# A kernel of seven-product projections on one Trainium2 core: another order of the products, x loaded by quarters, 1/rms moved into the functions, and branch work fed among the units

## The chip, the cores and the metric

The kernel runs on one core of one Trainium2 chip. The metric is the device time of one execution in microseconds (us). The figure for a kernel is the median of several runs; one further execution was taken with a profile, and every row below is from that one.

## What is computed

`x` is 512 tokens by 2048 channels, float32. It is normalised, projected by one large matrix, mixed in three branches, merged by gates, projected again and added to `x`:

```python
h = rmsnorm(x, norm_g)
a_u, a_b, a_c, a_z, b_v, b_g, b_z, c_u, c_z, gates = split(h @ w_in)   # nine of 1024 columns, gates 3 x 2048
y_a = (silu(a_z) * a_b * conv3(a_c * a_u)) @ w_br_a
v   = silu(layernorm(conv31(b_v * sigmoid(b_g)) + conv_b, ln_g, ln_b))
y_b = (silu(b_z) * v) @ w_br_b
y_c = (silu(c_z) * pool_mix(c_u) * scale) @ w_br_c                      # causal means of 2, 4, 8, 16
g   = sigmoid(gates)
x   = x + (g[0] * y_a + g[1] * y_b + g[2] * y_c) @ w_o
return rmsnorm(x, final_g)
```

## The kernel before

**Arithmetic.** Every matmul operand is split in a high part (rounded to the matmul's format) and a low part (the rest), and a product is three matmuls: high-high, low-high, high-low (L338, L339, L340 in a unit). Weights arrive as raw blocks of 128 x 1024. ScalarE (ACT) casts the high part `wh` (L125), VectorE (DVE) subtracts to get the low part `wl` (L126), both in halves of 512 columns.

**Units.** The input projection is cut into 15 units, each giving two column groups of 512. A unit computes a 2 x 2 block product by seven products instead of eight, named 11, s1, s2, s4, s3, 12 and 22 (`PRODUCTS`, L54). Each product runs over eight k, and at each k issues three matmuls to each of two PSUM banks: 48 matmuls a product, 336 a unit, all of 512 columns. Some blocks of raw weights are plain loads on SyncE's queue ("load", L105); others are added into the block before by an accumulating DMA that GpSimd issues ("add", L110). In the order before, the blocks that s1, s2 and s3 add to were begun four stages (of 1024 columns) earlier.

**Accumulation over products.** 11 is computed in the banks X, copied out by ACT (`snap`, L351), and s2 goes on in the same X; its sum is copied out, s3 goes on in X, and so does 22. s1 and s4 share the banks Z in the same way. Where a bank's contents are taken out, DVE's `join` (L360) or ACT's `snap` reads it before PE may write on. In the order before there is always a whole other product between two products on the same banks: 11 (X), s1 (Z), s2 (X), s4 (Z), s3 (X), 12 (V), 22 (X). 1/rms is applied as the scale of `snap` and `join`.

**Operands of x.** The seven left operands are built during unit 0 (`make`, L275, called by `run` at each k): x is loaded as 16 tiles `xa`, `xb` on SyncE's queue, scaled by `norm_g` on ACT, and combined and split on DVE. The token squares for 1/rms are loaded and summed in unit 0 too, since the first `join` needs 1/rms.

**What sets the order.** A queue of tasks (`todo`, and `urgent` ahead of it) holds all the other work: turning results to channels, the 31-tap convolution, LayerNorm, pooling. `feed` (L221) is called at each k of the products and hands out a number of tasks per call (`rate`). A scheduler then orders the instructions on each engine by priority; the split of weights has a high priority (L124). Each engine executes its queue in order.

**After the units.** Three branch products (`branch`, L633; branch 0 is y_a, 2 is y_c, 1 is y_b) and the output product `o`, whose last column group runs token block by token block (L829). The operands of branch 0 (`ua`) are loaded and halved after the last unit (L659 to L662); pooling and its mixing run as tasks during branch 0, the product silu(z)·v during branch 2. The units' order is glu, prod and side, pool, the six gate units, and `zed` last.

## Time and profile before

| | us |
|---|---|
| median of three runs | 1697.19 (1694.49 to 1698.14) |
| the profiled execution, its own time | 1691.05 |
| its span in the profile | 1689.3 |
| TensorE (PE) busy | 1642.6 (97%) |
| DVE busy | 1126.3 (67%) |
| ACT busy | 823.6 (49%) |

The span is the time from the first to the last instruction in the profile; the execution's own time has 1.75 us around it. PE's share says that almost all of the span is matmuls, and so the few per cent that are idle, or run at the lower clock, are where a change of schedule can act. The profile also gives the clock that TensorE was granted, as a share of its 2.4 GHz: 0.50 is 1.2 GHz.

### The profile page before, as it was taken

How to read it: one execution, taken by the hardware profiler on the slowest of the kernel's cores; microseconds unless marked ns; L12 is line 12 of the kernel's file. 1: busy time of each engine (PE TensorE's matmuls, PEld its weight loads, DVE VectorE, ACT ScalarE, POOL GpSimd, SP SyncE). 2: the span in 40 equal slices, each digit the busy share in tenths (PEclk: the TensorE clock that was granted, in tenths of full speed). 3: DMA queues.
4: the chain of work that ended last, by engine and by line, in shares of the span. 5: the costliest groups of instructions: out<-in, count | busy, mean ns of one | idle time of the engine just before them, and what ended most of it. 6: DMA issues, size and time to landing. Idle time of an engine off the chain costs nothing.

```text
span 1689.3 us, 21512 instructions
## 1 busy us (share of the span) xinstructions
PE 1642.6 (97%) x7332; PEld 1353.5 (80%) x7332; DVE 1126.3 (67%) x1873; ACT 823.6 (49%) x1436; POOL 208.3 (12%) x246
## 2 busy tenths in 40 slices
PE   5899999999999999899999999999899999999997
PEld 4688888888888888688888888888688888888886
DVE  4859989969987986775555555555666754453442
ACT  7855544544545555565555555555533322332332
POOL 1212111120302021212112030212000000000000
PEclk7999999999999999999999999999999999999999
DMA  9979898897989899999899898989854854443312
GB/s 313 224 217 202 214 217 174 198 235 198 169 228 208 239 225 272 259 272 223 220 224 214 235 203 236 203 239 215 284 168 130 287 182 145 128 131 100 89 61 100
DMA packets 114589, 341.31 MB, mean 202 GB/s; under 512 B 12720, under 2 KB 12848, under 8 KB 114480
## 3 DMA queue, kind: packets, MB, share of 16 engines
q0 software_dynamic: 34560, 125.84, 40.0%
q1 hardware_dynamic: 59616, 177.24, 32.8%
q10 hardware_dynamic: 20304, 36.87, 6.2%
q8 instruction: 57, 0.93, 0.2%
q14 instruction: 52, 0.43, 0.1%
HBM read 306.35 MB, written 33.55 MB: 201 GB/s over the span
## 4 chain that ended last, share of the span: by engine, by line
PE 92%; DMA 5%; DVE 1%; ACT 1%; issue 1%; SPq 0%; ACTq 0%; DVEq 0%
PE X L338 12%; PE X L339 12%; PE X L340 12%; PE Z L338 6%; PE Z L340 6%; PE Z L339 6%; PE y L642 5%; PE y L644 5%; PE y L643 5%; PE V L340 3%; PE V L338 3%; PE V L339 3%; PE o L810 3%; PE o L812 3%; PE o L811 3%; PE turned L431 2%
## 5 line engine op out<-in xcount | busy, mean ns | idle before, releaser
L126 DVE TENSOR_TENSOR wl<-rawA,wh 128x512 fp32r<-128x512 f32 x560 | 379.7, 687 | 263.3 <-ACT wh L125 227.8
L125 ACT CAST wh<-rawA 128x512 fp32r<-128x512 f32 x560 | 342.4, 621 | 393.3 <-PE X L339 88.9
L126 DVE TENSOR_TENSOR wl<-rawB,wh 128x512 fp32r<-128x512 f32 x320 | 217.9, 688 | 178.5 <-ACT wh L125 146.2
L125 ACT CAST wh<-rawB 128x512 fp32r<-128x512 f32 x320 | 196.1, 622 | 266.3 <-PE y L643 67.4
L110 POOL DMA_DIRECT2D rawA<-wts x180 | 155.7, 865 | 851.7 <-DVE wl L126 810.0
L338 PE MATMUL X<-wh,x 128*128 128x512 f32 x480 | 188.8, 396 | 14.3 <-ACT wh L125 10.8
L338 PE MATMUL X<-wh,xs 128*128 128x512 f32 x480 | 189.3, 394 | 11.5 <-ACT snap L351 5.8
L338 PE MATMUL Z<-wh,xs 128*128 128x512 f32 x480 | 187.4, 393 | 3.3 <-ACT xs L269 3.1
L339 PE MATMUL X<-wh,xs 128*128 128x512 f32 x480 | 188.4, 393 | 0.0
L339 PE MATMUL X<-wh,x 128*128 128x512 f32 x480 | 187.9, 392 | 0.0
L339 PE MATMUL Z<-wh,xs 128*128 128x512 f32 x480 | 187.6, 391 | 0.0
L340 PE MATMUL Z<-wl,xs 128*128 128x512 f32 x480 | 172.9, 391 | 0.8 <-DVE wl L126 0.8
L340 PE MATMUL X<-wl,x 128*128 128x512 f32 x480 | 172.2, 394 | 0.0
L463 DVE SCALAR_TENSOR_TENSOR conv<-v,prm,conv 128x511 f32<-128x511 f32 (+28 forms) x240 | 171.4, 727 | 0.0
L340 PE MATMUL X<-wl,xs 128*128 128x512 f32 x480 | 170.6, 393 | 0.1
L338 PEld LDWEIGHTS X<-wh,x 128*128 128x128 f32 x480 | 90.9, 190 | 34.6 <-ACT wh L125 12.0
L338 PEld LDWEIGHTS X<-wh,xs 128*128 128x128 f32 x480 | 91.1, 190 | 33.0 <-ACT wh L125 8.1
L125 ACT CAST wh<-rawC 128x512 fp32r<-128x512 f32 x120 | 71.5, 619 | 91.4 <-DMA rawC<-wts 43.4
L338 PEld LDWEIGHTS Z<-wh,xs 128*128 128x128 f32 x480 | 90.8, 189 | 22.9 <-ACT xs L269 3.5
L340 PEld LDWEIGHTS X<-wl,xs 128*128 128x128 f32 x480 | 90.8, 189 | 20.7 <-DVE wl L126 1.8
L340 PEld LDWEIGHTS Z<-wl,xs 128*128 128x128 f32 x480 | 90.6, 189 | 20.3 <-DVE wl L126 1.4
L339 PEld LDWEIGHTS X<-wh,xs 128*128 128x128 f32 x480 | 91.1, 190 | 18.9
(189 smaller groups left out, 2654.2 us busy)
## 6 DMA issues: line engine op xcount, KB each, us to landing
rawA<-wts POOLq DMA_DIRECT2D x180, 512.0 KB, 7.5
rawA<-wts SPq DMA_DIRECT2D x100, 512.0 KB, 4.4
rawB<-wts SPq DMA_DIRECT2D x100, 512.0 KB, 4.4
rawC<-wts SPq DMA_DIRECT2D x60, 512.0 KB, 4.2
rawB<-wts POOLq DMA_DIRECT2D x60, 512.0 KB, 7.1
g<-g SPq DMA_DIRECT2D x48, 256.0 KB, 4.4
g<-snap ACTq DMA_DIRECT2D x36, 256.0 KB, 4.0
xq<-xn SPq DMA_DIRECT2D x16, 256.0 KB, 7.2
```

The costliest lines, as they stand in the source:

```text
L110: self.nc.gpsimd.dma_start(out=t, in_=self.src[b], accum_op=ALU.add)
L125: self.nc.scalar.copy(out=h, in_=raw)
L126: self.nc.vector.tensor_tensor(out=l, in0=raw, in1=h.bitcast(F32), op=ALU.subtract)
L338: T.matmul(p, lhsT=xh, rhs=h, start=start and k == 0, stop=False, skip_group_check=True)
L339: T.matmul(p, lhsT=xl, rhs=h, start=False, stop=False, skip_group_check=True)
L340: T.matmul(p, lhsT=xh, rhs=l, start=False, stop=k == KB - 1, skip_group_check=True)
L463: V.scalar_tensor_tensor(out=c[:, s:], in0=v[:, : S - s], scalar=pcol(P_BW, i * CONV_B + CONV_B - 1 - s), in1=c[:, s:], op0=ALU.mult, op1= ...
L642: T.matmul(banks[t], lhsT=uh[:, tk], rhs=h, start=k == 0, stop=False)
L643: T.matmul(banks[t], lhsT=ul[:, tk], rhs=h, start=False, stop=False)
L644: T.matmul(banks[t], lhsT=uh[:, tk], rhs=l, start=False, stop=k == KB - 1)
L810: T.matmul(pt[t], lhsT=mh[:, tk], rhs=h, start=k == 0, stop=False)
L811: T.matmul(pt[t], lhsT=ml[:, tk], rhs=h, start=False, stop=False)
```

## The change

- `PRODUCTS` becomes 11, 12, s1, s4, s2, s3, 22. An added block now follows its predecessor by eight stages. The third pool of raw blocks is dropped, the second grows from 4 to 6.
- Weights are split by whole blocks of 1024 columns (the very first block in two pieces), two stages ahead; loads run four stages ahead instead of three.
- x comes by quarters (two k by 256 tokens): the two of the upper token half on ACT's queue at the start, the other two on SyncE's queue during the first products. Operands are built by pairs of k, up to four k ahead, with `norm_g` inside the instructions that split or subtract.
- 1/rms: `snap` is a plain copy, `join` a plain sum; the scale is applied in the sigmoids and products that follow. What follows the joins of unit 0 is put off to unit 1, where `roots` now runs; eight of the 16 squares move to unit 1.
- `feed` counts an estimate of VectorE's us per task: 0.5 us per k, 0.7 in the branches.
- `zed` comes ahead of the gate units. Pooling's mixing, the turning of z and the product silu(z)·v run among the gates' units; operands of branches 0 and 2 are loaded and halved in the last gate unit, those of branch 1 during branch 2.

The diff's core:

```diff
 PRODUCTS = (
     ("11", "A", "load", 0, 0),
+    ("12", "B", "load", 1, 0),
     ("s1", "A", "add", 0, 1),
+    ("s4", "B", "load", 1, 1),
     ("s2", "A", "add", 1, 1),
-    ("s4", "B", "load", 1, 1),
     ("s3", "B", "add", 0, 1),
-    ("12", "C", "load", 1, 0),
     ("22", "A", "add", 1, 0),
 )
...
+            pool, ht, lt = self.place(n_stage)
+            h = pool.tile([P, RAW], F32R, tag=ht, name=f"wh{n_stage}")
+            l = pool.tile([P, RAW], F32R, tag=lt, name=f"wl{n_stage}")
             with self.tc.high_priority(AHEAD):
-                self.nc.scalar.copy(out=h, in_=raw)
-                self.nc.vector.tensor_tensor(out=l, in0=raw, in1=h.bitcast(F32), op=ALU.subtract)
+                for at in self.pieces(n_stage):
+                    self.nc.scalar.copy(out=h[:, at], in_=raw[:, at])
+                    self.nc.vector.tensor_tensor(
+                        out=l[:, at], in0=raw[:, at], in1=h[:, at].bitcast(F32), op=ALU.subtract
+                    )
...
-    w = Weights(tc, nc, {"A": ra, "B": rb, "C": rc}, parts, wts, 3, 3)
-    xraw = []
-    for k in range(KD):
-        t = slot(F32, "xa") if k < KB else tmp("xb")
-        nc.sync.dma_start(out=t, in_=xT[:, k, :])
-        xraw.append(t)
-        if k in (0, 2, 4):
-            w.load_to(k // 2 + 1)
+    gcol = const.tile([P, KD], F32, name="gcol")
+    nc.scalar.dma_start(out=gcol, in_=par[:, P_G : P_G + KD])
+    w = Weights(tc, nc, {"A": ra, "B": rb}, parts, wts, 4, 2)
+    w.load_to(1)
+    for j in range(STEPS):
+        xload(nc.scalar, xa[j][:, :, half[0]], j, 0, 0)
+    for j in range(STEPS):
+        xload(nc.scalar, x12[j], j, 1, 0)
...
     def feed():
-        credit[0] += rate[0]
-        while credit[0] >= 1.0:
-            credit[0] -= 1.0
-            q = urgent or todo
-            if q:
-                q.popleft()()
+        credit[0] = min(credit[0] + rate[0], 2.0)
+        while credit[0] > 0.0 and (urgent or todo):
+            cost, f = (urgent or todo).popleft()
+            f()
+            credit[0] -= cost
...
+        def snap(banks):
+            ts = [tmp("snap") for _ in banks]
+            for p, t in zip(banks, ts):
+                A.copy(out=t, in_=p)
             return ts
+        def join(banks, ts, then):
             for i, (p, t) in enumerate(zip(banks, ts)):
-                s = col(r, i + 2 * half)
-                if first:
-                    A.activation(out=t, in_=t, func=AF.Copy, scale=s)
-                V.scalar_tensor_tensor(out=t, in0=p, scalar=s, in1=t, op0=ALU.mult, op1=ALU.add)
+                V.tensor_tensor(out=t, in0=p, in1=t, op=ALU.add)
                 then(i, t)
...
+    def first_each(n):
+        while makes and KD * len(sets) // 2 - 2 * len(makes) <= n + 4:
+            make(*makes.popleft())
+        if n in (2, 4, 6, 8):
+            j = n // 2 - 1
+            xload(nc.sync, x22[j], j, 1, 1)
+            xload(nc.sync, xa[j][:, :, half[1]], j, 0, 1)
+        if n == 10:
+            nc.sync.dma_start(out=prm, in_=par)
+        if n >= 32 and n % 3 == 2:
+            square(*squares_left.popleft())
...
+            def last_each(n):
+                if n == 18:
+                    halved_tasks(uad, ua)
+                    halved_tasks(ucd, uc)
...
-    ua = []
-    for i in range(KB):
-        t = fill(ud[i], "ua")
-        ua.append(halves(t, slot, "ua"))
```

**Start of the program, ACT's queue.** `wh` and `rawA` are the weights' high part and raw block, `xa` and `x_5` to `x_8` quarters of x, `x_17` and `x_21` first operands. Before:

```order
L185 DMA prm<-par 128x320
L204 ACT_TABLE_LOAD
L204 ACTIVATE s_129<-ones 128x1 [waits DVE_49]
L283 ACTIVATE xa_87<-xa_87,prm 128x512 [waits DMAHW1_49,DMAHW0_49]
L125 CAST wh_167<-rawA_89 128x512 [waits DMAHW2_49]
L125 CAST wh_171<-rawA_89 128x512
L283 ACTIVATE xa_91<-xa_91,prm 128x512 [waits DMAHW3_49]
L269 CAST x_21_162<-xa_87 128x256 [waits Activation_49]
```

After:

```order
L132 CAST wh_170<-rawA_93 128x512 [waits DMAHW2_49]
L205 DMA xa_83<-xT 128x2x256
L205 DMA xa_84<-xT 128x2x256
L205 DMA x_5_85<-xT 128x2x256 [waits DMAHW3_49]
L132 CAST wh_178<-rawA_162 128x1024 [waits DMAHW4_49]
L205 DMA x_6_86<-xT 128x2x256 [waits DMAHW5_49]
L205 DMA x_7_87<-xT 128x2x256 [waits DMAHW7_49]
L132 CAST wh_184<-rawA_164 128x1024 [waits DMAHW6_49]
L205 DMA x_8_88<-xT 128x2x256 [waits DMAHW1_49]
L225 ACTIVATE s_114<-ones 128x1 [waits DVE_49]
L307 ACTIVATE x_17_147<-xa_81,gcol 128x256 [waits DMAHW0_49]
```

The first operand stood behind one load and two casts; now six loads of x and three casts stand before it in these rows (the loads of `gcol` and two more of x, and a first cast, stand ahead of them), and the loads wait for lanes that earlier loads give back when they have landed (`DMAHW7` is that of `xa_83`, `DMAHW1` that of `xa_84`).

**The end of s3 in a quiet unit (the 13th), PE's queue.** `X`, `V` are PSUM banks, the `xs` and `x` operands. Before:

```order
L340 MATMUL X_8839<-wl_9249,xs_88_841 128x512 [waits DVE_49]
L338 MATMUL X_8840<-wh_9248,xs_88_841 128x512
L339 MATMUL X_8840<-wh_9248,xs_88_841 128x512
L340 MATMUL X_8840<-wl_9249,xs_88_841 128x512
L338 MATMUL V_9299<-wh_9260,x_91_863 128x512 [waits Activation_49]
```

After:

```order
L381 MATMUL X_7898<-wl_8299,xs_58_700 128x512
L379 MATMUL X_7899<-wh_8298,xs_58_700 128x512
L380 MATMUL X_7899<-wh_8298,xs_58_700 128x512
L381 MATMUL X_7899<-wl_8299,xs_58_700 128x512
L379 MATMUL X_7898<-wh_8316,x_59_720 128x512 [waits DVE_49,Activation_49]
L380 MATMUL X_7898<-wh_8316,x_59_720 128x512
```

The next product took other banks; now it takes the same bank again three matmuls after that bank's last one, and waits for DVE, whose `join` has to read it first. The scheduler then runs bank 0's matmuls of two blocks ahead of bank 1's.

**The same place in a unit with convolution (the fifth), DVE's queue, after the change.** `snap<-X` is the join; `conv` and `csum` are tasks of the convolution.

```order
L133 TENSOR_TENSOR wl_3139<-rawA_2534,wh_3138 128x1024 [waits DMASW4_49,PE_49,Activation_49]
L502 SCALAR_TENSOR_TENSOR conv_2603<-v_2579,prm,conv_2603 128x485 [waits DVE_49]
L133 TENSOR_TENSOR wl_3158<-rawA_2559,wh_3157 128x1024 [waits DMASW5_49,PE_49,Activation_49]
L515 TENSOR_TENSOR csum_2548<-csum_2548,conv_2581 128x512 [waits DVE_49]
L392 TENSOR_TENSOR snap_2939<-X_2672,snap_2939 128x512 [waits PE_49]
L392 TENSOR_TENSOR snap_2940<-X_2673,snap_2940 128x512 [waits PE_49]
L502 SCALAR_TENSOR_TENSOR conv_2603<-v_2579,prm,conv_2603 128x484 [waits DVE_49]
L133 TENSOR_TENSOR wl_3180<-rawA_2591,wh_3179 128x1024 [waits DMASW6_49,Activation_49]
```

Before, the join stood among splits and taps in the same manner (at half the width of a split), but PE's next product did not wait for it.

## Rows read from the trace of the kernel before

**Rows 1.** The page's first part: busy time, share of the span, instructions.

```profile
PE 1642.6 (97%) x7332; PEld 1353.5 (80%) x7332; DVE 1126.3 (67%) x1873; ACT 823.6 (49%) x1436; POOL 208.3 (12%) x246
```

**Rows 2.** Waits on PE: for what, us in total, times, longest.

```profile
PE X L338 <- ACT wh L125: 16.6, 7, 10.7
PE y L642 <- ACT uah L235: 5.9, 1, 5.9
```

**Rows 3.** Windows: us, busy of PE, PEld, DVE, ACT, POOL, clock, DMA share, GB/s.

```profile
8.20:36.20 28.00, 14.27 (x48) 10.94 (x48) 11.55 (x24) 21.45 (x47) 5.30 (x6) 0.74 1.05 335
...
62.50:65.90 3.40, 3.40 (x9) 2.63 (x8) 3.40 (x9) 3.40 (x10) 0.86 (x1) 0.50 0.72 110
112.90:659.40 546.50, 546.26 (x2452) 450.83 (x2451) 481.81 (x763) 277.33 (x468) 96.81 (x112) 1.00 0.91 213
659.40:748.10 88.70, 81.14 (x340) 64.17 (x339) 67.73 (x106) 53.35 (x90) 13.84 (x16) 0.96 0.99 272
...
686.50:693.50 7.00, 5.68 (x22) 3.45 (x21) 3.23 (x6) 4.57 (x9) 1.73 (x2) 1.00 1.05 258
...
748.10:1204.80 456.70, 456.70 (x2016) 378.30 (x2015) 257.15 (x378) 255.81 (x421) 82.17 (x95) 1.00 0.94 222
1204.80:1290.00 85.20, 79.28 (x361) 64.91 (x360) 51.27 (x99) 33.86 (x59) 0.00 (x0) 0.96 0.59 196
```

**Rows 4.** Timeline of unit 0: start, us, instruction [idle before <- releaser].

```profile
8.16 1.22 PE L338 MATMUL X<-wh,x 128*128 128x512 f32 x2 [3.42 <-ACT x L269]
...
17.88 0.33 SPq L105 DMA_DIRECT2D rawA<-wts  x1
...
28.69 0.80 PE L338 MATMUL X<-wh,x 128*128 128x512 f32 x1 [10.65 <-ACT wh L125]
```

**Rows 5.** DMA issues: count, KB each, median us from issue to landing.

```profile
rawA<-wts POOLq DMA_DIRECT2D x180, 512.0 KB, 7.5
...
xa<-xT SPq DMA_DIRECT2D x8, 256.0 KB, 5.9
...
prm<-par ACTq DMA_DIRECT2D x1, 160.0 KB, 4.1
```

**Rows 6.** Timeline of unit 0: runs of equal instructions on ACT and DVE.

```profile
6.05 1.14 ACT L125 CAST wh<-rawA 128x512 fp32r<-128x512 f32 x2 [0.36 <-DMA rawA<-wts]
6.70 1.29 DVE L126 TENSOR_TENSOR wl<-rawA,wh 128x512 fp32r<-128x512 f32 x2 [5.12 <-ACT wh L125]
...
32.48 2.09 DVE L287 TENSOR_TENSOR q<-xb,xa 128x256 f32<-128x256 f32 x6
...
35.30 0.57 ACT L349 COPY snap<-X 128x512 f32<-128x512 f32 x1
35.77 1.02 ACT L269 CAST xs<-q 128x256 fp32r<-128x256 f32 x3
```

**Rows 7.** Timeline at the end of s3 in the fifth unit (convolution).

```profile
404.91 0.62 PE L340 MATMUL X<-wl,xs 128*128 128x512 f32 x2
...
405.36 0.62 PE L340 MATMUL V<-wl,x 128*128 128x512 f32 x2
...
405.82 1.41 DVE L360 SCALAR_TENSOR_TENSOR snap<-X,Rn,snap 128x512 f32<-128x512 f32 x2
```

**Rows 8.** Timeline at the end of the last unit and the start of branch 0.

```profile
1204.13 0.39 PE L340 MATMUL X<-wl,x 128*128 128x512 f32 x1
...
1204.56 0.69 ACT L617 ACTIVATE c<-X,Rp 128x512 f32<-128x512 f32 x1 [0.28 <-PE X L340]
...
1210.45 1.27 ACT L235 CAST uah<-ua 128x512 fp32r<-128x512 f32 x2 [2.93 <-DMA ua<-ua]
...
1211.12 2.08 PE L642 MATMUL y<-wh,uah 128*128 128x512 f32 x4 [5.92 <-ACT uah L235]
```

**Rows 9.** Timeline of the ninth unit, in which LayerNorm runs.

```profile
688.63 0.50 PE L338 MATMUL X<-wh,xs 128*128 128x512 f32 x1 [0.59 <-ACT wh L125]
...
713.06 0.80 PE L338 MATMUL X<-wh,xs 128*128 128x512 f32 x1 [5.77 <-ACT snap L351]
```

More of the change, by code (lines that the diff above doesn't have):

```diff
@@ L80, in stages @@
     for u in range(len(UNITS)):
-        for _, tag, what, row, col in PRODUCTS:
-            out += [(tag, (u, tag, s), what, block(u, row, col, s)) for s in range(STEPS)]
+        for name, tag, what, row, col in PRODUCTS:
+            key = (u, tag, name == "12")
+            out += [(tag, key + (s,), what, block(u, row, col, s)) for s in range(STEPS)]
     for n, b in enumerate(range(BR_AT, N_BLOCK)):
@@ new lines, in trunk, with operand, quarter @@
+    qs = [None] * STEPS
+    def operand(name, j, src):
+        t = sets[name][j] = slot(F32R, f"x{name}")
+        A.copy(out=t[:, :, half[0]], in_=src)
+        V.tensor_tensor(out=t[:, :, half[1]], in0=src, in1=t[:, :, half[0]].bitcast(F32), op=ALU.subtract)
+    def quarter(name, j, src, rows):
+        t = sets[name][j] = slot(F32R, f"x{name}")
+        for c in range(2):
+            g = gcol[:, KB * rows + 2 * j + c :][:, :1]
+            h, l = t[:, c, half[0]], t[:, c, half[1]]
+            A.activation(out=h, in_=src[:, c], func=AF.Copy, scale=g)
+            V.scalar_tensor_tensor(
+                out=l, in0=src[:, c], scalar=g, in1=h.bitcast(F32), op0=ALU.mult, op1=ALU.subtract
+            )
@@ L282, in make, with less @@
+    def less(out, in0, in1, j, rows, gs):
+        for c in range(2):
+            V.scalar_tensor_tensor(
+                out=out[:, c], in0=in0[:, c], scalar=gs[:, KB * rows + 2 * j + c :][:, :1], in1=in1[:, c],
+                op0=ALU.mult, op1=ALU.subtract,
+            )
+    def make(name, j):
+        x11, x21 = xa[j][:, :, half[0]], xa[j][:, :, half[1]]
         if name == "11":
-            A.activation(out=xa, in_=xa, func=AF.Copy, scale=pcol(P_G, k))
-            operand(name, k, xa[:, half[0]])
+            quarter(name, j, x11, 0)
+        elif name == "12":
+            quarter(name, j, x12[j], 1)
@@ L301, in make @@
-            operand(name, k, xa[:, half[0]])
-        else:
-            operand(name, k, xb[:, half[name == "22"]])
+            less(x11, x11, x21, j, 0, gcol)
+            operand(name, j, x11)
+        else:
+            quarter(name, j, x22[j], 1)
+    makes = deque((p[0], j) for p in PRODUCTS for j in range(STEPS))
     squares = const.tile([P, 4 * NT], F32, name="squares")
@@ L364, in unit @@
         run("11", X, True)
-        a = snap(X, Rp, 0)
+        a = snap(X)
+        U = [psum("V") for _ in range(2)]
+        run("12", U, True)
+        join(U, a, on11)
         Z = [psum("Z") for _ in range(2)]
         run("s1", Z, True)
-        e = snap(Z, Rn, 1)
+        e = snap(Z)
+        run("s4", Z, False)
         run("s2", X, False)
-        u = snap(X, Rn, 0)
-        run("s4", Z, False)
-        if first:
-            roots()
-        join(Z, Rn, 0, u, on12)
+        u = snap(X)
@@ L514, in spread, with act_tasks, load @@
             var.clear()
+        add(0.7, average)
+        add(0.0, conv_load, 0)
+        add(1.0, lambda: None)
+        for i in range(KB):
+            if i + 1 < KB:
+                add(0.0, conv_load, i + 1)
+            add(1.4, center, i)
+        add(3.5, spread)
+    def act_tasks():
+        z = {}
+        def load(i):
+            conv_load(i)
+            z[i] = fill(zd[i], "z")
         def act(i):
@@ new lines, in second_each, with delayed, put, on21 @@
+    def second_each(n):
+        if n % 2 == 0 and squares_left:
+            square(*squares_left.popleft())
+        if n == 18:
+            roots()
+        if n >= 20 and late:
+            late.pop(0)()
+    def delayed(hooks):
+        def put(f):
+            return lambda *args: late.append(lambda: f(*args))
+        def on21(t, p):
+            o = tmp("c21")
+            A.copy(out=o, in_=p)
+            late.append(lambda: hooks["on21"](t, o))
+        return dict({k: put(f) for k, f in hooks.items()}, on21=on21)
@@ L626, in trunk @@
+            unit(**kept(left, right)[0], **(dict(each=last_each) if c == 5 else {}))
     flush()
```

527 lines of the change are left out of this document (256 added, 271 removed).

## The prediction

> **What bounds the kernel now.** I read the page's busy shares first: PE has 97% of the span [rows 1], so a change of schedule can win at most what is idle on PE or runs at the lower clock. The windows say where that is [rows 3]. From 748.1 to 1204.8 us, six units, PE is busy in all of 456.7 us at clock 1.00: 76.1 us a unit, or 336 matmuls of 0.2265 us. That is the floor of a unit. From 112.9 to 659.4 PE is busy in 546.26 of 546.5. The loss lies in four places. Unit 0, which ends where that row begins, takes 112.9 − 8.2 = 104.7 us, 28.6 over the floor; in its first 28 us PE is busy for 14.27, at clock 0.74. The ninth unit, with LayerNorm, takes 88.7, 12.6 over the floor. At the start of branch 0 PE is idle for 5.9 us, and the clock of that window is 0.96. And the first real matmul starts only at 8.16. The waits name two causes [rows 2]: weights not yet cast, 16.6 us, and `ua` not yet halved, 5.9. So PE is the bound, and DVE (67%) comes next: in the convolution's units it is busy 481.8 of 546.5 us, 88%.
>
> **First matmul: +5.3 us.** Before, it starts at 8.16 [rows 4]. Now ACT's queue holds six loads of x ahead of the first operand; the last two wait until `xa_83` and `xa_84` have landed, and ACT issues these only after its first casts. Before, such a pair of casts ran from 6.05 to 7.19 [rows 6]; with fewer loads ahead on SyncE's queue I put the issue of `xa_83` at 6.0 to 6.6. Landing takes between 4.1 us (one early load) and 5.9 (the median of `xa`) [rows 5]; one issue and two short ACT instructions follow, about 1 us. So the first matmul lies between 6.0 + 4.1 + 1 = 11.1 and 6.6 + 5.9 + 1 + 0.4 (the second landing) + 1.0 (a cast of 1024 columns) = 14.9. I take 13.5, nearer the upper end, since the queue of loads is as long as that of the median `xa`.
>
> **Unit 0: −18.1 us.** The stall of 10.65 us that ends at 28.69 is for a weight block issued only at 17.88, behind the loads of `xb` on SyncE's queue [rows 4]. Now seven weight blocks stand ahead of x on that queue and half of x is on ACT's: this stall goes, and the lower clock that followed it. What is late next is DVE. Started back to back, 512 columns take 0.60 on DVE (two end after 1.29, the last of them 0.69 long), 256 columns 0.335 (six in 2.09); 1024 columns then take about 1.14, an estimate along the same line, and at most 1.20 (two of 512). On ACT 512 columns take 0.52, 256 columns 0.31, and so 1024 about 0.96 [rows 6]. In the two products s1 and s4 (16 k, 21.8 us of PE) DVE must do 24 combinations of 256 columns (8.0 us), 8 splits of x of 512 (4.8), 8 splits of weights (9.1) and two joins (1.2): 23.1 us, more than 21.8. It works in a fixed order, so each late operand stops PE. Followed through the two queues with these durations, PE stops for about 3, 4.3 and 1.5 us in s1, s4 and s2: 8.8. The idle before the first matmul costs clock, as the row from 62.5 shows such a spell: 3.4 us at 0.50 [rows 3], 1.7 lost. Unit 0 then takes 76.1 + 8.8 + 1.7 = 86.6 instead of 104.7. Bounds: 78 (only the clock is lost) and 95 (each stall twice as long).
>
> **Units 1 to 14: +4.6.** *What goes:* most of the ninth unit's 12.6 us. It lost 5.77 at 713.06 behind a burst of LayerNorm's work on ACT and DVE, idles such as the 0.59 at 688.63, and clock [rows 9]. LayerNorm is now spread by a budget of 0.5 us per k, and accumulated blocks are issued a stage earlier and eight stages after their base; GpSimd's loads need 7.5 us to land [rows 5], and four stages are 10.9 us. I leave 2 us: −10.6. *What comes:* three hand-overs a unit in which the next product needs the same banks at once. The last matmul on a bank is followed by three on the other, so PE wants the bank 4 × 0.2265 = 0.91 after that matmul's start. Whoever empties the bank starts 0.43 after it (1204.13 to 1204.56), and PE goes on 0.05 after the emptying ends (1210.45 plus one cast, 0.62, to 1211.12) [rows 8]. A plain copy on ACT takes 0.57 [rows 6], a sum on DVE 0.69 like a split of 512. So s1 to s4 and s2 to s3 wait 0.43 + 0.57 + 0.05 − 0.91 = 0.14 us each if ACT is free, s3 to 22 waits 0.26 if DVE is free. But DVE is not free in the units with convolution. In the fifth unit the join after s3 started at 405.82, though its bank was ready at 404.91 + 0.43 = 405.34, and PE went on at 405.36 only because its next matmul had other banks [rows 7]. With the same lateness PE would now wait until 405.82 + 0.74 + 0.05 = 406.61, for 1.25 us. I take 0.26 in seven quiet units (1.8) and 0.6 to 1.8, by the place of the join among splits and taps, in seven others (9.5): 11.3; and 14 × 0.28 = 3.9 for the ACT hand-overs. 15.2 − 10.6 = +4.6. Bounds: −10.6 if the scheduler's turns between the banks cover all of it, +19 if DVE is late by a split and a tap (1.14 + 0.65, on top of 0.26) in all 14.
>
> Splitting by 1024 columns, the plain snap and join and the moved scales save DVE some 28 × 0.06 us and a little more a unit; PE does not wait for that, so 0. The price is that a split of 1024 may stand in front of a join; it is in the 1.8 and in the bound. Squares, `prm` and `roots` moved to unit 1: 0, since nothing before the joins of unit 1 needs them.
>
> **Start of branch 0: −9.1.** The operands are halved in the last gate unit, so the 5.92 us [rows 8] go, and the lower clock after them: 4% of 79.28 busy us [rows 3], 3.2. In exchange, 16 loads, casts and splits lie in the last unit, where ACT and DVE were busy for 56% of the time [rows 3]; a cast that waits for its load holds ACT's queue, which I price at 0, at most 3 us.
>
> **The sum.** 5.3 − 18.1 + 4.6 − 9.1 = −17.3, from the profiled execution's 1691.05: 1673.8. The median of the runs lies 6.1 above that execution, so I forecast **1680** (−1.0%).
>
> **The rivals.** *A: slower, because DVE empties X too late after s3.* Each of 15 units has one such hand-over, in front of which PE has no other work. The sum holds 11.3 us for them; the gain is used up when they cost 11.3 + 17.3 = 28.6, or 1.9 us a unit: a split of 1024 and a tap in front of each join. For it: DVE is 88% busy in the convolution's units, and was 0.48 late where nothing pressed [rows 3, 7]. Against: a late join stops PE, and so gives DVE time to catch up; the quiet units have no taps. At 2.5 us a unit it is 37.5 − 11.3 = +26: 1706. *B: the start gains little.* ACT's queue waits in order for landings, so the next blocks' `wh` are late, and unit 0 still takes 97 us after a first matmul at 15: 12 more, 1692. For it: the block of rows 4 took about 10 us to land, under the same early crowd of loads. *C: the hand-overs cost nothing*, covered by the turns between banks: 15 less, 1665. *D: the clock falls at each hand-over.* In the trace the idle of 0.59 at 688.63 lies in a stretch whose granted clock is 1.00, while the idle of 3.42 before 8.16 is followed by two matmuls in 1.22 us, the lower level [rows 3, 4, 9]. If each of 45 hand-overs were followed by 1.7 us of loss, the time would be 1680 + 76 = 1756; the stretch around 688.63 speaks against it. The Trainium skill has a rule that speaks for it: "TensorE: Matmul & The Clock Gate", section "A second HAM failure mode: psum-queue depth-cycling", tells of a kernel whose short PE idles between matmul groups, as it cycled through PSUM banks, made the clock swing between its two levels; by that rule this change would be a clear loss. *E: the halved operands come too late*, as tasks at the end of the queue: +9, so 1689.
>
> **How the numbers follow.** About 0.2% (3.4 us) is what a measurement of this kernel can tell from no change. Chances: forecast 0.55, B 0.14, E 0.05, C 0.09, A 0.14, D 0.03. Faster are the forecast, C, E and half of B, with what of A stays short of its point: 0.78. The same: the rest of B and A's weak end, 0.09. Slower: most of A, and D, 0.13. The range leaves out D, most of A and the far end of C. Low end: 1680 − 9 (unit 0 at 78) − 10 (two thirds of C) = 1661. High end: 1680 + 8 (unit 0 at 95) + 1.4 (first matmul at 14.9) + 3 (last unit) + 5 (joins half as late again) = 1697. The forecast's own range is 1669 to 1690.
>
> One rule bears on the first matmul. The Trainium skill's "DMA: Bandwidth & Descriptors", in its summary table, says that spreading loads over the issuing engines gives no bandwidth and saves only issue time. By that rule x would land no sooner from ACT's queue, and the first matmul would lie at the late end of the bounds given; no row of this trace shows it.
>
> **What would show it.** First matmul near 13.5, behind ACT's wait for `xa_83`; no stall of 10 us on `wh` in the first 40 us; unit 0 ended near 100; as the largest waits left, some 45 short ones of PE on `snap` and on DVE's join, 0.15 to 2 us each, at clock 1.00; the LayerNorm unit under 80; branch 0 starting at the last unit's end. It is wrong if PE waits on the join for over 28 us in sum (A), if the clock is under 1.00 in quiet units (D), or if unit 0 ends after 108 (B).

## The result, and the profile after

The changed kernel takes 1736.2 us (median of four runs, 1735.4 to 1738.9) where the kernel before takes 1695.8: 2.4% slower, a ratio of 1.024 with an interval of 1.0222 to 1.0258. The forecast was 1680, with a range of 1661 to 1697. The profiled execution has a span of 1733.7 us instead of 1689.3: 44.4 more. The windows of the changed kernel, cut at the unit boundaries (columns as in [rows 3]); the first two are the start and unit 0, which is the first of the fifteen; from here on units are counted from one, as in the prediction's "ninth unit", and the third row holds units 2 to 9; then come the tenth to twelfth, the two quiet ones, the last, and all that follows:

```profile
0.00:22.20 22.20, 3.79 (x16) 3.49 (x16) 4.69 (x23) 5.25 (x8) 3.43 (x9) 1.00 0.95 294
22.20:116.40 94.20, 85.07 (x337) 66.61 (x338) 68.05 (x105) 56.75 (x97) 12.21 (x15) 0.95 0.83 214
116.40:766.90 650.50, 638.57 (x2850) 520.96 (x2849) 510.58 (x615) 303.86 (x356) 110.71 (x129) 0.99 0.87 204
766.90:860.20 93.30, 85.61 (x380) 69.11 (x379) 60.29 (x73) 51.84 (x68) 14.52 (x17) 0.96 0.96 262
860.20:946.90 86.70, 83.83 (x367) 68.47 (x366) 63.71 (x101) 41.72 (x51) 13.11 (x16) 1.00 0.95 249
946.90:1038.00 91.10, 82.78 (x349) 66.54 (x348) 58.08 (x69) 43.37 (x52) 13.81 (x17) 0.94 0.96 262
1038.00:1192.60 154.60, 154.21 (x673) 125.69 (x673) 76.49 (x68) 74.84 (x85) 27.69 (x33) 1.00 0.93 218
1192.60:1282.00 89.40, 81.20 (x339) 65.28 (x338) 48.28 (x50) 46.15 (x59) 12.85 (x15) 0.94 0.93 239
1282.00:1733.70 451.70, 443.01 (x2032) 368.94 (x2030) 187.75 (x257) 112.93 (x151) 0.00 (x0) 1.00 0.43 136
```

Against [rows 3, 4]: the first matmul comes 14.0 us later (22.2 instead of 8.2); unit 0 is 10.5 shorter (94.2 instead of 104.7); the other fourteen units take 1165.6 instead of 1091.9, 73.7 more; what follows takes 451.7 instead of 484.5, 32.8 less. In sum 44.4. About 150 matmuls moved from the branches into the units (pooling's 48 of 512 columns at 0.227 us, and some 100 short turnings that follow each other at 0.11): by this estimate 22 us that only change place. Without them the fourteen units lost 52 us, and the branches won 11.

PE's waits of the changed kernel, to be set beside [rows 2]:

```profile
PE X L379 <- ACT wh L132: 19.0, 5, 7.3
PE X L379 <- ACT x L307: 17.3, 1, 17.3
PE X L379 <- DVE snap L392: 12.9, 12, 2.9
PE Z L379 <- ACT wh L132: 3.8, 3, 1.7
PE X L381 <- DVE wl L133: 3.7, 3, 2.2
```

Three kinds are to be seen: the start (17.3), the join after s3 (12.9, twelve times), and weights not yet split (26.5 by three rows), although there are now more loads ahead. The last kind is what the forecast did not have. Two timelines show what lies behind it. In the twelfth unit, on SyncE's queue, DVE, ACT and PE:

```profile
1005.67 0.44 SPq L191 DMA_DIRECT2D c<-cd  x1
...
1019.10 0.69 DVE L572 TENSOR_TENSOR c<-c,rstd 128x512 f32<-128x512 f32 x1 [10.08 <-DMA c<-cd]
...
1020.55 1.03 ACT L132 CAST wh<-rawB 128x1024 fp32r<-128x1024 f32 x1
...
1021.63 0.79 PE L379 MATMUL X<-wh,xs 128*128 128x512 f32 x1 [7.32 <-ACT wh L132]
```

This load is one of LayerNorm's second pass, which the change joins with the product with z; from its issue to the instruction that reads it went 13.4 us. DVE stood before it for 10.1, ACT behind DVE, and the weight cast that PE needed behind both. In the last unit ACT stands before operands of branch 2 in the same way, and a row of the DMA issues says that these loads took 15.7 us in the median:

```profile
1246.63 0.62 ACT L262 CAST u<-u 128x512 fp32r<-128x512 f32 x1 [2.65 <-DMA u<-uc]
...
1251.92 0.79 PE L379 MATMUL X<-wh,xs 128*128 128x512 f32 x1 [5.50 <-ACT wh L132]
```

```profile
u<-uc SPq DMA_DIRECT2D x8, 256.0 KB, 15.7
```

### The profile page after: what moved, and what is told of

Same layout as the page of the kernel before. It is cut to its first block, busy times and chain, and to the rows that moved or that the text cites. A ratio compares the mean times of both kernels' runs of the same rounds, so it can differ in the third digit from the quotient of the medians.

```text
span 1733.7 us, 19754 instructions
## 1 busy us (share of the span) xinstructions
PE 1658.1 (96%) x7332; PEld 1355.1 (78%) x7332; DVE 1077.9 (62%) x1360; ACT 736.7 (42%) x919; POOL 208.3 (12%) x246
## 4 chain that ended last, share of the span: by engine, by line
PE 83%; DMA 8%; DVE 4%; ACT 2%; issue 1%; SPq 0%; ACTq 0%; DVEq 0%
PE X L379 11%; PE X L380 10%; PE X L381 10%; PE Z L379 5%; PE Z L380 5%; PE Z L381 5%; PE y L816 5%; PE y L815 5%; PE y L814 5%; PE V L380 3%; PE V L379 3%; PE V L381 3%; PE o L888 3%; PE o L890 3%; PE o L889 3%; DVE wl L133 2%
## 5 line engine op out<-in xcount | busy, mean ns | idle before, releaser
L133 DVE TENSOR_TENSOR wl<-rawA,wh 128x1024 fp32r<-128x1024 f32 (+1 forms) x281 | 341.8, 1218 | 251.2 <-ACT wh L132 247.6
L132 ACT CAST wh<-rawA 128x1024 fp32r<-128x1024 f32 (+1 forms) x281 | 294.5, 1049 | 435.6 <-PE X L380 146.2
L133 DVE TENSOR_TENSOR wl<-rawB,wh 128x1024 fp32r<-128x1024 f32 x220 | 268.4, 1222 | 285.5 <-ACT wh L132 284.4
L132 ACT CAST wh<-rawB 128x1024 fp32r<-128x1024 f32 x220 | 231.2, 1053 | 343.8 <-PE y L815 106.5
L379 PE MATMUL X<-wh,x 128*128 128x512 f32 x480 | 191.5, 400 | 33.6 <-ACT x L307 17.3
L379 PE MATMUL X<-wh,xs 128*128 128x512 f32 x480 | 192.3, 401 | 20.0 <-ACT wh L132 18.1
L381 PE MATMUL X<-wl,x 128*128 128x512 f32 x480 | 179.7, 397 | 0.0
L381 PE MATMUL X<-wl,xs 128*128 128x512 f32 x480 | 175.9, 397 | 3.8 <-DVE wl L133 3.7
L502 DVE SCALAR_TENSOR_TENSOR conv<-v,prm,conv 128x511 f32<-128x511 f32 (+28 forms) x240 | 165.6, 726 | 0.1
L814 PE MATMUL y<-wh,u 128*128 128x512 f32 x384 | 149.9, 390 | 0.0
L815 PE MATMUL y<-wh,u 128*128 128x512 f32 x384 | 149.7, 390 | 0.0
L816 PE MATMUL y<-wl,u 128*128 128x512 f32 x384 | 149.5, 390 | 0.0
L379 PEld LDWEIGHTS X<-wh,xs 128*128 128x128 f32 x480 | 91.7, 191 | 46.8 <-ACT wh L132 20.0
```

The lines of the kernel that those rows point to most:

```text
L132: self.nc.scalar.copy(out=h[:, at], in_=raw[:, at])
L133: self.nc.vector.tensor_tensor(out=l[:, at], in0=raw[:, at], in1=h[:, at].bitcast(F32), op=ALU.subtract)
L379: T.matmul(p, lhsT=xh, rhs=h, start=start and k == 0, stop=False, skip_group_check=True)
L381: T.matmul(p, lhsT=xh, rhs=l, start=False, stop=k == KB - 1, skip_group_check=True)
L502: V.scalar_tensor_tensor(out=c[:, s:], in0=v[:, : S - s], scalar=pcol(P_BW, i * CONV_B + CONV_B - 1 - s), in1=c[:, s:], op0=ALU.mult, op1= ...
L814: T.matmul(banks[t], lhsT=uh[:, tk], rhs=h, start=k == 0, stop=False)
```

## The experiments

Three theories were set against each other, the first two from the start, the third after the first four runs (x on SyncE's queue, the two runs with earlier loads, and the old order). **Q**: queues that work in order stand behind single loads that were issued too late. **H**: the hand-overs between products on the same banks. **D**: the units have hardly any room on the DMA engines (share 0.91 to 0.99 in [rows 3]), and the change moved loads and stores out of the branches, which have (0.43 above).

### Loads issued in another place or earlier: theory Q fails

**Loads of x on SyncE's queue.**

```diff
-        xload(nc.scalar, xa[j][:, :, half[0]], j, 0, 0)
+        xload(nc.sync, xa[j][:, :, half[0]], j, 0, 0)
...
-        xload(nc.scalar, x12[j], j, 1, 0)
+        xload(nc.sync, x12[j], j, 1, 0)
```

> The changed kernel, with the eight loads of x at the start issued on SyncE's queue instead of ACT's; nothing else. In the changed kernel the first matmul started at 22.2 us, behind ACT's queue: the loads of the later quarters of x stood in it ahead of the first operand and waited for lanes until 21.1. Theory Q (queues that work in order stand behind late loads): the first operand is ready when its own quarter has landed, first matmul at 6 to 9 us; the weight blocks now come behind eight loads of x, so PE waits for the second block, some 5 us of the gain go back; 1724 to 1730 us against 1736. Theory H (the hand-overs between products on the same banks cost what was lost): the start is no more than a shift, unit 0 ends where it ended (116 us), 1733 to 1738.

1736.1 us, ratio to before 1.0255 (1.0232 to 1.0277). The first matmul came at 6.55, 15.7 earlier, and unit 0 ended at 113.6 instead of 116.4. Of 15.7 us 12.9 came back: PE was idle in unit 0 for 20.0 us instead of 9.1, and its matmuls took 2 us more. Windows of this run:

```profile
6.50:45.00 38.50, 28.79 (x106) 22.57 (x107) 25.27 (x44) 22.18 (x38) 4.07 (x6) 0.82 1.05 340
45.00:113.60 68.60, 58.33 (x233) 44.84 (x232) 45.54 (x65) 36.97 (x61) 10.53 (x13) 0.95 0.76 178
```

Up to 45 us the DMA share is 1.05, at 340 GB/s, and the waits that came (9.6 us) are for weight blocks, which now stand behind the loads of x: the engines are full, whatever the queue. After 45 us the share is 0.76, and the 10.3 us that PE is idle there are not explained by full engines.

**Branch operands, and LayerNorm's loads, fetched tasks ahead.**

```diff
+        for i in range(3):
+            add(0.0, ufetch, d, i)
+        add(2.0, lambda: None)
         for i in range(KB):
-            add(0.7, halved, d, u, i)
+            if i + 3 < KB:
+                add(0.0, ufetch, d, i + 3)
+            add(0.7, halved, u, i)
```

> The changed kernel, with each load of a branch operand issued three tasks ahead of its halving, instead of in the same task. In the changed kernel the last unit took 89.1 us with two waits of PE for a weight cast (2.5 and 5.5 us), while ACT stood before a cast of a branch operand that waited for its load. Theory Q: the casts find their data, these two waits go and the clock lost behind them, the last unit takes 77 to 80 us; 1725 to 1729 us against 1736. Theory H: the last unit stays over 86, 1734 to 1738.

1735.3 us, 1.0255 (1.0234 to 1.0276): no change. The last unit took 88.4; issued earlier, the loads took longer, 17.1 us in the median instead of 15.7. The edit for LayerNorm is the same, in its two loops:

> The changed kernel, with LayerNorm's loads issued three tasks ahead (centring) and two tasks ahead (the product with z) instead of one. In the changed kernel DVE stood 10.1 us before such a load in the twelfth unit and 5.5 us in the tenth; the tenth to twelfth unit took 93.3, 86.7 and 91.1 us. Theory Q: the wait of 7.3 us of PE in the twelfth unit goes and the waits of the tenth shrink; the three units take together 252 to 262 us instead of 271; 1722 to 1728 us against 1736. Theory H: they stay within 3 us, 1733 to 1738.

1731.9 us, 1.0237 (1.0216 to 1.0258). The twelfth unit went from 91.1 to 88.3 and the tenth from 93.3 to 89.8, the eleventh from 86.7 to 90.2: 268 in sum, not 252 to 262. So for these loads it is not that they are issued too late.

### Transfers in the units: theory D

**Dummy loads in the kernel before.**

```diff
+            def extra():
+                x = tmp("xd")
+                nc.sync.dma_start(out=x, in_=xn[0, :, :CH])
+
+            todo.extend([extra] * {1: 8, 2: 16, 3: 24, 4: 32}.get(c, 0))
             unit(False, **kept(left, right)[0])
```

> The kernel before, with extra loads of 256 KB that nothing reads, issued on SyncE's queue as tasks among the gate units: 8 in the eleventh unit, 16 in the twelfth, 24 in the thirteenth, 32 in the fourteenth, none in the tenth. These units had a DMA share of 0.94 and took 76.16 us each. Theory D: what fits in the remaining share is free, the rest lengthens the unit: at the 250 to 270 GB/s seen where the share is near 1.0, the eleventh unit 76 to 77 us, the twelfth 78 to 82, the thirteenth 84 to 90, the fourteenth 91 to 98; 1725 to 1745 us. Theory H: loads that no engine waits for cost nothing, all of them within 1 us of 76.2; 1694 to 1699.

1738.4 us, 1.027 (1.0242 to 1.0298). The expectation miscounted by one: the units with 8, 16, 24, 32 and no loads are the tenth to fourteenth. Their windows, in this order:

```profile
751.80:829.30 77.50, 77.50 (x338) 62.51 (x337) 40.91 (x62) 40.65 (x71) 13.87 (x16) 1.00 0.99 247
829.30:911.00 81.70, 79.62 (x338) 62.04 (x337) 40.42 (x62) 39.97 (x71) 13.87 (x16) 1.00 0.99 258
911.00:998.00 87.00, 81.66 (x337) 62.95 (x336) 40.49 (x62) 39.87 (x71) 13.87 (x16) 0.98 0.98 265
998.00:1097.20 99.20, 83.42 (x338) 63.09 (x338) 40.62 (x63) 40.62 (x71) 13.87 (x16) 0.93 0.97 250
1097.20:1173.30 76.10, 76.10 (x337) 63.04 (x336) 42.45 (x62) 42.72 (x71) 13.88 (x16) 1.00 0.93 221
```

No engine reads these loads, and all the other work is that of the kernel before. Eight cost 1.3 us, 16 cost 5.5, 24 cost 10.8, 32 cost 23: within the expected ranges for the second and third dose, 0.5 and 1.2 us over them for the first and last. From the second dose on each load of 256 KB costs 0.5 to 1.5 us; at the 258 GB/s of the second row its bytes alone are 1.0. One rival is left in this run, since SyncE's queue also issues weights. Its waits, dummy loads first, weights second:

```profile
SPq L615 <- DMA xd<-xn: 68.9, 31, 3.0
SPq L105 <- DMA xd<-xn: 14.5, 8, 4.8
```

So weight loads did stand behind dummy loads. Up to 24 loads the rate rises with the dose (221, 247, 258, 265 GB/s), as it would if bytes set the time; with 32 it falls to 250, so that some 6 of those 23 us (an estimate: the unit's bytes at 265 GB/s would take 94) go to the queue or to waits.

**Branch work back in the branches**, with the old order of products and then with the new one:

```diff
-                for gi in range(len(WINDOWS)):
-                    pool_tasks(gi)
...
-            add(0.0, act_tasks)
...
-                    halved_tasks(ucd, uc)
...
-    rate[0] = 0.7
+    rate[0] = 1.4
+    for gi in range(len(WINDOWS)):
+        pool_tasks(gi)
+    add(0.0, halved_tasks, ucd, uc)
     branch(0, ua)
     flush()
...
-    halved_tasks(ubd, ub)
+    act_tasks()
+    add(0.0, halved_tasks, ubd, ub)
     branch(2, uc)
```

Both runs also issue the branch operands' loads three tasks ahead and double the tasks' budget in the branches (0.7 to 1.4). `act_tasks` holds LayerNorm's second pass, which the kernel before ran in its ninth unit, so a little more than the moved work goes to the branches. What goes back is the work of DVE and ACT together with its transfers; these runs don't part the two.

> The changed kernel with the old order of products (as in the run with the old order), and the pooling tasks and the product with z put back into branches 0 and 2, where the DMA share is under 0.5; only the operands of branch 0 are loaded and halved in the last unit, each load three tasks ahead. Theory D: the eleventh to fourteenth unit take 76 to 78 us each instead of 86.7, 87.8, 76.2 and 76.2, the last 77 to 80, the branches grow by the 20 us of matmuls that come back to them; 1676 to 1688 us, under both kernels. Theory H: the place of the branch work does not matter, 1697 to 1702.

1681.5 us, 0.9931 (0.9914 to 0.9948), faster than both kernels. The tenth unit, the eleventh to fourteenth, the last, and what follows:

```profile
746.20:832.80 86.60, 83.05 (x373) 68.10 (x372) 54.70 (x59) 49.83 (x65) 13.84 (x17) 0.98 0.97 261
832.80:1137.50 304.70, 304.70 (x1346) 252.28 (x1345) 153.14 (x136) 149.39 (x169) 55.42 (x65) 1.00 0.94 223
1137.50:1214.30 76.80, 76.73 (x338) 62.81 (x337) 42.52 (x42) 40.86 (x51) 12.80 (x15) 1.00 0.98 244
1214.30:1677.70 463.40, 454.69 (x2081) 377.95 (x2079) 242.32 (x381) 129.98 (x179) 0.00 (x0) 1.00 0.50 166
```

Four units at the floor, 76.2 each; the last at 76.8 although it still loads and halves the eight operands of branch 0; branches at a share of 0.50 take the rest without a wait of PE. The tenth unit, with LayerNorm's first pass alone, keeps 86.6 us at a DMA share of 0.97: 10.4 over the floor, 4 of them turnings, although no branch work is left in it. With the new order:

> The changed kernel with its new order of products, and only the branch work put back into the branches (as in the run that put it back with the old order; there it won 18 us). Theory S (two separate losses, hand-overs and DMA room): about the same again, the eleventh and twelfth unit at 77.3 us like the quiet ones and the last at 78 to 80; 1705 to 1718 us. Theory M (the hand-overs only make each late transfer cost more, and are cheap by themselves): with the transfers gone the loss to the old order is under 8 us, 1682 to 1690.

1703.9 us, 1.0052 (1.0033 to 1.0072): 32 under the changed kernel, as separate losses give. Units 2 to 15 take 1126.2 us instead of 1165.6; of these 39.4, 11 are matmuls that moved, 28 are waits and slow matmuls that went.

### The order of products: theory H

**The old order in the changed kernel**, and the new order in the kernel before; the edit shown is the table. The sequence of `run` and `join` in `unit` and the building of the operands follow it; in the changed kernel loads also go three stages ahead instead of four, and what follows the join of Z is put off behind 12.

```diff
-    ("12", "B", "load", 1, 0),
     ("s1", "A", "add", 0, 1),
-    ("s4", "B", "load", 1, 1),
     ("s2", "A", "add", 1, 1),
+    ("s4", "B", "load", 1, 1),
     ("s3", "B", "add", 0, 1),
+    ("12", "B", "load", 1, 0),
     ("22", "A", "add", 1, 0),
```

> The changed kernel with the order of products of the kernel before (11, s1, s2, s4, s3, 12, 22), loads three stages ahead instead of four (accumulated blocks need it), and what follows the join of Z put off behind 12. All else stays as changed. The waits of PE on the join after s3 were 12.9 us in sum, those at the two ACT hand-overs some 0.3 us a unit. Theory H: with no product behind another on the same banks, the units 1 to 14 lose all of the 54 us that they gained over the kernel before; 1685 us or less. Theory Q: the quiet units go from 77.3 to 76.2, and the join's waits go with the clock lost behind them, 18 to 26 us in all, while the start, the LayerNorm units and the last unit keep their stalls; 1710 to 1718 us.

1699.3 us, 1.0038 (1.002 to 1.0057): 37 less, between the two theories. All waits on the join are gone, the quiet units are at 76.2. The tenth to twelfth unit still take 88.8, 86.7 and 87.8, with the DMA share at 0.97 to 1.01 (H had wanted all of the units' loss back):

```profile
746.70:835.50 88.80, 84.13 (x376) 68.42 (x376) 58.38 (x71) 49.74 (x64) 13.85 (x16) 0.98 0.97 256
835.50:922.20 86.70, 85.16 (x370) 68.70 (x369) 62.90 (x102) 42.29 (x52) 13.83 (x16) 1.00 0.99 266
922.20:1010.00 87.80, 82.95 (x349) 67.18 (x349) 59.36 (x73) 43.77 (x52) 13.88 (x16) 0.96 1.01 276
```

> The kernel before with the new order of products (11, 12, s1, s4, s2, s3, 22) and nothing else of the change; what follows the join of 12 is put off behind the join of Z, and in the first unit the join of 12 stands behind s4, since 1/rms is not known earlier. Theory H (hand-overs): putting the old order into the changed kernel won 37 us, so putting the new one into the kernel before should lose about as much: units 1 to 14 longer by 20 to 35 us in sum, the quiet units 77.2 to 77.5 us instead of 76.2; 1712 to 1730. Theory D (DMA: the units have little room on the DMA engines, and the moved branch work fills it): the order alone costs only its own waits, 10 to 15 us; 1704 to 1709.

1763.4 us, 1.0405 (1.039 to 1.0421): 69 more, far over both. Its waits on the join are 20.7 us, its quiet units 78 us; but 21 us of waits on snaps and 29 on weights (17 before, [rows 2]) came too, in the first and the LayerNorm unit above all. Why the kernel before suffers so much more was not followed up; it splits by 512 columns, scales in its snaps and joins, and counts tasks instead of time. In its quiet units PE waits 0.7 us for each join, where the changed kernel waits 0.2.

**Loads three stages ahead** in the changed kernel (`4, 2` to `3, 2`):

> The changed kernel with loads three stages ahead instead of four; nothing else. The run with the old order had to make this change too, so it tells whether the depth of the loads took part in the 37 us that were won there. If the order alone won them: 1733 to 1741 us. If the depth did: under 1728.

1733.6 us, 1.0239 (1.0205 to 1.0273), in the range expected if the order alone won: the depth took no part that can be told from noise.

**One hand-over alone.** Table and sequence 11, 12, s1, s2, s4, s3, 22:

> The kernel of the run with the old order and the branch work back (1681.5 us), with the order 11, 12, s1, s2, s4, s3, 22: of the three hand-overs of the changed kernel only s3 to 22, by DVE's join, is left; loads stay three stages ahead. Theory S: the join's waits come back, 0.2 to 0.4 us in quiet units, 0.7 to 2.9 in the convolution's, 12 to 16 in sum with the clock; 1692 to 1699 us. If the two copies by ACT carry the loss instead: under 1687.

1691.7 us, 0.9981 (0.9967 to 0.9994), 10 over the run with the old order and the work back. The whole hides two parts: unit 0 ended 10.4 us earlier (105.5 instead of 115.9), and units 2 to 15 took 1120.7 instead of 1098.4, 22.3 more. The two ACT hand-overs add only 5.5 to that (1126.2 with all three). Units 2 to 15 with the old order, with one hand-over, and with three:

```profile
115.90:1214.30 1098.40, 1093.90 (x4902) 903.35 (x4901) 758.56 (x852) 541.85 (x638) 192.77 (x223) 1.00 0.91 220
105.50:1226.20 1120.70, 1100.20 (x4902) 904.90 (x4901) 760.24 (x852) 543.87 (x638) 192.74 (x223) 1.00 0.91 216
115.80:1242.00 1126.20, 1108.98 (x4906) 903.91 (x4905) 762.40 (x852) 546.36 (x639) 192.71 (x223) 1.00 0.90 215
```

Unit 0 tells another story: it takes 83.9 us here and 93.7 with all three hand-overs, so there the place of s4 ahead of s2 costs 9.8. The join's waits, 15.8 us in sum:

```profile
PE X L379 <- DVE snap L392: 15.8, 15, 3.7
```

**The join and the copies first** (`with tc.high_priority(2 * AHEAD)` around both, in the changed kernel):

> The changed kernel, with the copies and sums that empty a bank (snap and join) given a higher priority than the splits of weights in the order of ACT and DVE. Theory H: the 12.9 us that PE waited for the join after s3 fall to the 0.2 us each that are left with DVE free, and the time falls by 10 to 20; 1716 to 1726. Theory D: the waits shorten, but in the units whose DMA share is at 0.95 and over PE waits for its weights instead; 1726 to 1734.

1736.5 us, 1.0244 (1.0229 to 1.026), waits on the join 13.0. It tests nothing: around the joins after s3 DVE ran the same order of instructions as without. DVE is late by its backlog. In the changed kernel's sixth unit, DVE and then PE:

```profile
505.64 1.11 DVE L495 TENSOR_SCALAR conv<-v,prm 128x512 f32<-128x512 f32 x2 [0.70 <-DMA v<-d]
506.67 1.22 DVE L133 TENSOR_TENSOR wl<-rawA,wh 128x1024 fp32r<-128x1024 f32 x1
507.81 1.41 DVE L502 SCALAR_TENSOR_TENSOR conv<-v,prm,conv 128x511 f32<-128x511 f32 x2
509.13 1.22 DVE L133 TENSOR_TENSOR wl<-rawA,wh 128x1024 fp32r<-128x1024 f32 x1
510.26 0.74 DVE L502 SCALAR_TENSOR_TENSOR conv<-v,prm,conv 128x510 f32<-128x510 f32 x1
510.92 0.69 DVE L392 TENSOR_TENSOR snap<-X,snap 128x512 f32<-128x512 f32 x1
```

```profile
508.05 0.39 PE L381 MATMUL X<-wl,xs 128*128 128x512 f32 x1
...
508.73 0.39 PE L381 MATMUL X<-wl,xs 128*128 128x512 f32 x1
511.75 0.76 PE L379 MATMUL X<-wh,x 128*128 128x512 f32 x1 [2.63 <-DVE snap L392]
512.32 0.63 PE L380 MATMUL X<-wh,x 128*128 128x512 f32 x1
```

From 505.64 on DVE has no gap. Bank 0's last matmul started at 508.05, so the bank was ready near 508.5; the rest of a tap, a split and another tap still stood in front. The wait costs more than its 2.63 us: in the 3.4 us that follow the granted clock is 0.50, the lower level, and matmuls start 0.43 apart instead of 0.227.

**No tasks before the join.**

```diff
-                feed()
+                if name != "s3" or k < 3:
+                    feed()
```

> The kernel of the run with one hand-over (1691.7 us), with no tasks handed out in the last five k of s3; all else the same. PE waited 15.8 us for the join after s3, 0.2 in units without tasks for DVE. Theory A (tasks of the convolution stand in DVE's queue in front of the join): these waits fall to 3 to 8 us, 1682 to 1687. If the wide splits alone make the join late: 13 us and more stay, 1690 to 1694.

1689.4 us, 0.9973 (0.9961 to 0.9986), not clear of 1691.7; the waits on the join are 15.5. They fell in every other unit to the least, and stayed in those between:

```profile
255.26 0.47 PE L379 MATMUL X<-wh,x 128*128 128x512 f32 x1 [3.00 <-DVE snap L393]
335.45 0.47 PE L379 MATMUL X<-wh,x 128*128 128x512 f32 x1 [0.20 <-DVE snap L393]
416.05 0.47 PE L379 MATMUL X<-wh,x 128*128 128x512 f32 x1 [2.40 <-DVE snap L393]
496.27 0.47 PE L379 MATMUL X<-wh,x 128*128 128x512 f32 x1 [0.20 <-DVE snap L393]
```

Where DVE had caught up, the wide splits do no harm; where it had not, tasks handed out before still stand there. So neither expectation is met as it stands. That the amount of work per k is at fault, and not its place, is my reading; no run changed the amount.

### The start, and a version that beats both

**x and weights by turns on SyncE's queue**, on the run with the old order and the work back:

```diff
     for j in range(STEPS):
-        xload(nc.scalar, xa[j][:, :, half[0]], j, 0, 0)
-    for j in range(STEPS):
-        xload(nc.scalar, x12[j], j, 1, 0)
+        xload(nc.sync, xa[j][:, :, half[0]], j, 0, 0)
+        w.load_to(j + 2 if j < 3 else 4)
...
```

> The kernel of the run with the old order and the branch work back (1681.5 us), with the first four quarters of x on SyncE's queue, one after each weight block, and the four of the other half from the twelfth k on. First matmul at 6 to 8 us instead of 19.6. Theory W (the start waits for its place in ACT's queue): unit 0 ends at 103 to 109 us instead of 115.9; 1669 to 1675 us. Theory D (in the first 45 us the DMA engines are full, so an earlier start only waits elsewhere): unit 0 ends at 112 to 116; 1677 to 1682 us.

1679.5 us, 0.9907 (0.9882 to 0.9932), not clear of 1681.5. The other four loads of x go out from the twelfth k on. First matmul at 6.9, unit 0 ended at 114.3 instead of 115.9: as D has it.

**The new order's first half in unit 0 alone** (11, 12, s1, s2, s4, s3, 22), the old order in all others:

```diff
+FIRST = tuple(PRODUCTS[i] for i in (0, 5, 1, 2, 3, 4, 6))
...
-        for name, tag, what, row, col in PRODUCTS:
+        for name, tag, what, row, col in PRODUCTS if u else FIRST:
```

> The kernel of the run with the old order and the branch work back (1681.5 us), with the order 11, 12, s1, s2, s4, s3, 22 in the first unit alone. With that order in all units the first unit took 83.9 us after a first matmul at 21.6, with the old order 96.3 after 19.6. Theory N (the first unit is set by when each quarter of x is needed: 12 ahead of s1 gives the two late quarters 11 us more): it ends at 104 to 108 us instead of 115.9, all other units stay; 1669 to 1676 us. Theory D alone (transfers fill the start whatever the order): 112 to 116, 1678 to 1684.

1675.3 us, 0.9896 (0.9877 to 0.9915): the lowest of all, though not clear of 1679.5. Unit 0 takes 84.0 us and ends at 105.4, though it starts only at 21.4. The other units did not stay as they were: units 2 and 3 took 78.9 and 85.4 instead of 76.5 and 80.0, so that of the 10.5 us won 6 are left in the time.

```profile
0.00:21.40 21.40, 3.83 (x17) 3.53 (x17) 4.75 (x23) 5.31 (x8) 3.44 (x9) 0.69 0.93 292
21.40:105.40 84.00, 79.82 (x337) 64.01 (x338) 67.34 (x105) 56.77 (x97) 12.23 (x15) 0.98 0.93 242
```

With the old order PE waited for an operand of s1, which needs the two late quarters of x; with 12 ahead of it that wait is gone:

```profile
PE Z L379 <- ACT xs L299: 11.3, 1, 11.3
```

(that row is of the run with the old order and the branch work back). So it is both: the first 45 us are full of transfers, and within that it counts which bytes are needed first.

## Why the prediction was wrong, point by point

- **First matmul, +5.3: measured +14.0.** The mechanism was right (ACT's queue behind the landing of `xa_84`), the landing mis-sized: bounds of 4.1 and 5.9 us from single rows [rows 5], measured 15.4 (issued at 5.68, landed at 21.1). The upper bound for the first matmul, 14.9, was passed by 7.3. The DMA share of 1.05 in the first window of [rows 3] said that all loads would share the engines.
- **Unit 0, −18.1: measured −10.5.** Both first terms together were forecast to end unit 0 at 100; it ended at 116.4. The stalls have the forecast size, 9.1 us for 8.8 (3.7 in s1, 2.3 in s4, 2.7 in s3 and 0.3 behind it), though only 2.6 of them end with DVE and 4.8 with a weight cast. Mis-sized are the slow matmuls behind the waits, the lower clock above all: PE was busy for 85.1 us on what takes 76.1 at the floor, 9 where I had 1.7. That a short unit 0 was to be had shows in the runs with s2 ahead of s4: 83.9 and 84.0 us.
- **Hand-overs, 15.2 within units 1 to 14 of the forecast's numbering.** The rule of lateness held: 12.9 us of waits on the join against 11.3 forecast. But the effect of the hand-overs was about twice the 15.2: taking all of them away won 33.6 us in these units (the old order in the changed kernel) or 27.8 (with the branch work back), 22.3 of it by the join. The quiet units show the least of it: 77.3 instead of 76.2, 1.1 us for three hand-overs where 0.54 was forecast, and only 0.2 of that stands as a wait; the rest is in matmuls that take longer. Fourteen times that is 15 of the 27.8; the join's waits beyond 0.2 are 9 more, and the lower clock behind the long ones some 3 (10.2 us at 0.50 instead of 3.4). The upper bound of +19 for these units was low too: its own terms add up to 22.
- **"I leave 2 us" for LayerNorm, and the last unit's operands "at 0, at most 3 us": the step that failed.** The tenth to twelfth and the last unit took 93.3, 86.7, 91.1 and 89.4, some 40 us in all over the floor and their moved matmuls. I counted the moved work on DVE and ACT, by a budget in VectorE's us, and never asked what its loads and stores find on the DMA engines, though [rows 3] had 0.94 to 0.99 where the work went and 0.59 where it came from. The dummy loads price it: 24 in a unit cost 10.8 us. By the rates of the windows these four units moved as much more than a quiet unit as 29, 18, 27 and 17 such loads, which by the doses would cost about 47 us: an estimate, near the 40. It fits transfers as the cause; that the moved work of DVE and ACT has no part in it was not tested by itself. Some 6 of the 40 are LayerNorm's own: the tenth unit kept them when the branch work was gone. I had read the ninth unit's 12.6 us as a burst on ACT and DVE that a budget would spread, and passed over the DMA share of 0.99 in its row of [rows 3].
- **Branch start, −9.1: measured about −11** with the moved matmuls taken off. Right: no wait of PE is left there.
- **Rival A** (the join late by over 28.6 us) did not come by its own sign, 12.9 us of waits; but the join's whole effect, 22.3, is most of the way there. **B** did, in effect: the start gained nothing, 3.5 us were lost. **C** did not, since the hand-overs cost 27.8 and more. **E** did not come at the start of branch 0; the late operands stopped the last unit instead. **D** did not come for the short idles: the quiet units' window has clock 1.00 with three hand-overs each. Behind long ones it came in part: after the join's waits of 2.18 us at 267.92 and 2.63 at 511.75 the clock was 0.50 for 3.4 us, after 2.87 at 935.91 it stayed at 1.00. The Trainium skill's "TensorE: Matmul & The Clock Gate", section "A second HAM failure mode: psum-queue depth-cycling", tells of such swings; this trace does not agree for idles of 0.2 us; the clock of 0.50 stands behind two of the twelve waits on the join alone. The Trainium skill's "DMA: Bandwidth & Descriptors", in its summary table, says that spreading loads over issuing engines gives no bandwidth; this case agrees: unit 0 ended at 113.6 and 116.4 with x on SyncE's or ACT's queue, at 114.3 and 115.9 in the other pair.
- **No rival had the right place.** The sum by the runs: order and moved work cost 56 us together in the fourteen units (33.6 + 22.7, or 27.8 + 28.5 if the moved work is taken away first), the start 3.5, less 11 for the branches: 49, where 44.4 was measured; with both undone these units are a few us better than before.

What stays open: why the new order costs the kernel before 69 us, how much of the order's cost is waits that only arise because DVE is full, and how the loss by the moved work divides between bytes, their order in SyncE's queue, and work of DVE and ACT.

## What to carry to other kernels

Before moving work under cover of another stage, read every resource of that stage, the share of the DMA engines too: here a stage with PE at 100% and DMA at 0.94 had cover for some eight loads of 256 KB (1.3 us) and no more, with DVE busy for little over half of it. The loads that landed late in such a stage were not mended by issuing them earlier; taking the work to another stage did help. And two products that follow each other on the same accumulator bank make a backlog of the engine that empties it a wait of the matmuls; here a product on other banks in between was worth 28 to 34 us, and one stage more or less between loads nothing that could be measured.

## What the hardware showed beyond that

The quiet units' steady stream, weights with the gates' own loads and stores, holds the DMA engines at a share of 0.94 and 222 GB/s; adding loads, the share rose to 0.99 and the rate to 258 to 265 GB/s, and then the unit grew instead. In the first 45 us the same engines moved 299 to 343 GB/s at a share of 1.05 (x by turns with weights, and the fastest run), so a full share does not mean one rate. And the same eight loads of branch 2's operands landed in 15.7 us in the median in the changed kernel's last unit, and in 5.7 in the branches at a share of 0.50.
